# Float32r weight units of 1024 columns, Winograd products accumulated in PSUM, a second tile written ahead of the norm's sum, in a hybrid decoder layer on one core

## The chip, the cores and the metric

The kernel runs on one core of a Trainium2 chip. The metric is the device time of one execution in microseconds (us), lower is better. Engines are named as in the profile: PE is TensorE (PEld its weight loads), DVE is VectorE, ACT is ScalarE, POOL is GpSimd and SP the queue that issues most DMAs.

## The reference

One decoder layer over 512 tokens of width 1024, in float32:

```python
x = x + 0.5 * swiglu(rms_norm(x, ffn1_norm), w_gate, w_up, w_down)     # FFN1, inner width 2816
h = rms_norm(x, mix_norm)
proj = h @ w_in                                                        # RWKV, attention and gate columns
y_rwkv = rwkv7_branch(...)                                             # a recurrence over the tokens, 8 heads of 64
y_att  = attention_branch(...)                                         # sliding window of 128, 8 query heads, 2 key heads
merged = gate_rwkv * (y_rwkv @ w_branch_rwkv) + gate_att * (y_att @ w_branch_attn)
x = x + merged @ w_out
x = x + 0.5 * swiglu(rms_norm(x, ffn2_norm), w_gate2, w_up2, w_down2)  # FFN2
x = rms_norm(x, final_norm)
# swiglu(h) = (silu(h @ w_gate) * (h @ w_up)) @ w_down
```

## The kernel before

**Stages.** The five stages follow each other on the core: the start (transposes of x, the norm's sum, the first FFN1 tiles), FFN1, mix1 (projections, the RWKV recurrence and attention, interleaved), mix2 (branches, gates, `w_out`), FFN2 with the final norm. Activations are kept transposed, features on the 128 partitions and 512 tokens along a row, as eight tiles.

**Products in three passes.** Every float32 product is three float32r matmuls (`mm3`): high part by high part, and the low part of each factor by the high part of the other. So each weight tile is loaded raw (`wr`, or `wx`), its high part `wh` is cast on ACT (L176) and its low part `wl`, raw minus high, is subtracted on DVE (L177, in `split_w`). A raw unit holds `WU` = 512 columns on 128 partitions, 256 KB, and each of the tags `wr`, `wh`, `wl` has three buffers for each of two streams, "a" and "b" (gate and up weights, or even and odd tiles).

**FFN tiles.** The inner width of an FFN is 22 tiles of 128 features. Most are made in pairs (`PAIRS`: 9 pairs in FFN1, tiles 4 to 21, and 11 in FFN2, all tiles). `ffn_pair` makes a pair's gate and up by a scheme of seven products in place of eight (Strassen and Winograd): tokens in two halves of 256, the contraction in two, the two tiles of the pair as two. Sums of the activations (`block_sums`, tags `xt`, `th`, `tl`) are made once for each FFN and shared by its pairs; sums of the weights (`S`, in `wx` buffers) are made for each pair, at L399: four sums, of which `SUMS = (1, 0, 1, 1)` puts three on POOL and one on DVE, each done for gate and for up. A pair's seven products are each 24 matmuls of 256 columns for gate and up together, 168 in all. Each product has its own PSUM tile (`sm`); seven additions on DVE (L399, `xt<-s,sm` and the like) and one copy on ACT (L416) combine them into `x0` and `x1`. `act` then multiplies by the norm's factor `rs` (L449), applies SiLU on ACT (L451), multiplies gate by up (L452) and splits the result into `h` (cast L204, subtraction L205).

**The start.** FFN1's first four tiles are made singly, with 48 matmuls of 512 columns each (eight contraction tiles by three passes, for gate and for up). The first tile's matmuls are written between the transposes of x. The second's weights are loaded and split early (`nextw`); its matmuls are written in `ffn_h`, behind `rs_finish`, which sums the squares over the features with a matmul against ones (L291) and makes `rs` from it. The scheduler may still place matmuls ahead of the sum, as the order below shows. Tiles three and four follow, then the pairs.

**Order.** Where the code sets `pe, v, s` to `InOrder`, the instructions keep the order in which they are written; elsewhere a scheduler places each instruction by its own estimates. In mix1 the matmul jobs (`JOBS`) run in one lane beside lanes for the recurrence and attention; a job's weights are split `AHEAD` = 4 units before use, and `LOE = (1, 0, 0)` puts one in three of their low subtractions on POOL in place of DVE.

## Time and profile before

| what | before |
|---|---|
| device time, median of three runs | 1190.36 us |
| the three runs | 1187.4, 1190.36, 1190.53 us |
| profiled execution: its time | 1189.17 us |
| profiled execution: span in the trace | 1187.4 us |
| mean granted clock of TensorE | 0.987 of full speed |
| busy PE, DVE, ACT, POOL over the span | 1138.7 (96%), 936.5 (79%), 603.7 (51%), 296.2 (25%) us |
| matmuls | 7386 |

The span is the profiled execution from its first to its last instruction; the 1.8 us between it and the execution's time lie around it. PE is busy for nearly the whole span, so the question in each stage is how often PE stood still, and at what rate its matmuls started. Busy shares are averages over stages that have different limits. Records of pipelined matmuls overlap, so the rate of a stretch is read from the number of matmuls that started in it.

### The profile page before, as it was taken

Reading aid. Unit: us, or ns where it says so; the run is one execution under the profiler, and the core shown is the slowest. Engines: PE = TensorE matmul, PEld = TensorE weight load, DVE = VectorE, ACT = ScalarE, POOL = GpSimd, SP = SyncE. Lnnn points to the kernel's source line nnn. Section 1 sums busy time; section 2 is a strip of 40 time slices with the busy share of each in tenths; the row PEclk is TensorE's granted clock in tenths of the full one; section 3 lists DMA queues with packets and bytes.
Section 4 is the critical chain, followed back from the end, with each engine's and each line's share of the span. In section 5 each row is a group of like instructions: output and inputs, shape, how many; then the busy total and the mean of one; then the engine's idle time right before and its main releaser. Section 6 shows DMA issues by size and latency. Waiting matters only on the chain.

```text
span 1187.4 us, 20295 instructions
## 1 busy us (share of the span) xinstructions
PE 1138.7 (96%) x7386; PEld 959.6 (81%) x7386; DVE 936.5 (79%) x1544; ACT 603.7 (51%) x1215; POOL 296.2 (25%) x260
## 2 busy tenths in 40 slices
...
GB/s 235 51 90 146 68 81 102 130 107 81 74 105 170 172 136 57 107 69 95 105 89 136 91 149 113 233 159 66 90 115 134 80 72 94 127 119 81 80 107 71
DMA packets 224597, 130.16 MB, mean 110 GB/s; under 512 B 39248, under 2 KB 205969, under 8 KB 224497
## 3 DMA queue, kind: packets, MB, share of 16 engines
...
q14 instruction: 43, 0.34, 0.1%
...
## 4 chain that ended last, share of the span: by engine, by line
PE 69%; DVE 20%; issue 4%; ACT 3%; DMA 3%; SPq 0%; POOL 0%; DVEq 0%; ACTq 0%; POOLq 0%
PE sm L201 12%; PE sm L200 12%; PE sm L199 11%; PE mm L199 9%; PE mm L200 9%; PE mm L201 8%; PE sm L78 5%; DVE wl L177 5%; DVE pr L916 2%; DVE wx L399 1%; PE sm L68 1%; DVE xt L399 1%; DVE t L449 1%; DVE t L452 1%; ACT wh L176 1%
## 5 line engine op out<-in xcount | busy, mean ns | idle before, releaser
L176 ACT CAST wh<-wr 128x512 fp32r<-128x512 f32 (+1 forms) x282 | 172.1, 612 | 245.4 <-PE mm L200 104.7
L177 DVE TENSOR_TENSOR wl<-wr,wh 128x512 fp32r<-128x512 f32 (+1 forms) x257 | 202.2, 791 | 91.0 <-ACT wh L176 90.3
L399 POOL TENSOR_TENSOR wx<-wr,wx 128x512 f32<-128x512 f32 x80 | 127.8, 1598 | 350.5 <-DVE wl L177 209.1
L176 ACT CAST wh<-wx 128x512 fp32r<-128x512 f32 x200 | 120.6, 619 | 141.5 <-PE sm L200 56.3
L201 PE MATMUL sm<-th,wl 128*128 128x256 f32 x640 | 181.6, 284 | 9.9 <-DVE wl L177 9.8
L199 PE MATMUL sm<-th,wh 128*128 128x256 f32 x640 | 180.2, 282 | 0.0
L200 PE MATMUL sm<-tl,wh 128*128 128x256 f32 x640 | 180.2, 282 | 0.0
L177 DVE TENSOR_TENSOR wl<-wx,wh 128x512 fp32r<-128x512 f32 x200 | 164.2, 851 | 14.2 <-ACT wh L176 14.2
L199 PE MATMUL sm<-xh,wh 128*128 128x256 f32 (+2 forms) x536 | 159.5, 298 | 0.0
L201 PE MATMUL sm<-xh,wl 128*128 128x256 f32 (+2 forms) x536 | 158.4, 296 | 0.6 <-DVE wl L68 0.3
L200 PE MATMUL sm<-xl,wh 128*128 128x256 f32 (+2 forms) x536 | 158.2, 295 | 0.5 <-DVE xl L263 0.5
L199 PE MATMUL mm<-xh,wh 128*128 128x512 f32 x304 | 128.1, 421 | 2.7 <-DVE g L1270 2.1
L201 PEld LDWEIGHTS sm<-th,wl 128*128 128x128 f32 x640 | 120.5, 188 | 12.5 <-DVE wl L177 12.5
L200 PE MATMUL mm<-xl,wh 128*128 128x512 f32 x304 | 124.5, 410 | 0.0
L201 PE MATMUL mm<-xh,wl 128*128 128x512 f32 x304 | 123.5, 406 | 0.0
L199 PEld LDWEIGHTS sm<-th,wh 128*128 128x128 f32 x640 | 120.7, 189 | 0.0
L200 PEld LDWEIGHTS sm<-tl,wh 128*128 128x128 f32 x640 | 120.6, 188 | 0.0
L200 PEld LDWEIGHTS sm<-xl,wh 128*128 128x128 f32 (+1 forms) x536 | 102.6, 191 | 4.2 <-issue 0.8
L201 PEld LDWEIGHTS sm<-xh,wl 128*128 128x128 f32 (+1 forms) x536 | 102.6, 191 | 4.0 <-DVE wl L68 0.8
L199 PEld LDWEIGHTS sm<-xh,wh 128*128 128x128 f32 (+1 forms) x536 | 102.7, 192 | 3.6 <-issue 0.8
L399 POOL TENSOR_TENSOR wx<-wx 128x512 f32<-128x512 f32 x40 | 60.0, 1500 | 113.4 <-DMA wx<-in_ffn_w_gate_dram 75.3
L199 PEld LDWEIGHTS mm<-xh,wh 128*128 128x128 f32 x304 | 58.1, 191 | 19.5 <-issue 2.6
...
## 6 DMA issues: line engine op xcount, KB each, us to landing
...
```

Of the source, the lines that this page charges most:

```text
L68: return lambda *a, **k: self.tc.keep_in_program_order(f(*a, **k))
L78: self.pe.matmul(out, lhsT=lhsT, rhs=rhs, **k)
L176: s.copy(out=hi[:, :n], in_=raw[:, :n])
L177: (e or v).tensor_tensor(out=lo[:, :n], in0=raw[:, :n], in1=hi[:, :n].bitcast(F32), op=ALU.subtract)
L199: pe.matmul(acc, lhsT=ah, rhs=bh, start=(first and k == 0), stop=False)
L200: pe.matmul(acc, lhsT=ah, rhs=bl, start=False, stop=False)
L201: pe.matmul(acc, lhsT=al, rhs=bh, start=False, stop=(last and k == n - 1))
L399: e.tensor_tensor(out=o, in0=a, in1=b, op=op)
L449: v.tensor_tensor(out=sv, in0=gate, in1=rs if len(gate.shape) == 2 else rs.rearrange("p (a c) -> p a c", a=2), op=ALU.mult)
L452: v.tensor_tensor(out=sv, in0=sv, in1=up, op=ALU.mult)
L916: v.tensor_tensor(out=pv_[:, m], in0=a_[:, m].unsqueeze(2).broadcast_to(sh), in1=b_[:, m].rearrange("p u c -> p c u").unsqueeze(1).broadca ...
```

## The change

Four edits go together.

1. A weight unit holds 1024 columns. In a pair it holds a product's gate and up weights side by side; in single tiles all eight contraction tiles; in FFN2's down product two tiles. The two streams become one, with three buffers of each kind (the same bytes). `wx` goes from six buffers of 512 to five of 1024. Units shorter than 1024 columns (w_branch_rwkv, w_branch_attn) leave the rest of their buffer unused.
2. In a pair, products that share an addend are accumulated in one PSUM tile (`pa` takes four products, `pc` two, `pb` one). Copies of the intermediate states of `pa` and `pc` are made on ACT, and three additions on DVE remain. The order of the products changes, and the sign of one activation sum with it.
3. The second tile's 48 matmuls are written as `pnext` ahead of `rs_finish`, into PSUM tiles of another tag (`mm`).
4. In mix1 a job's weights are one unit in place of two, `AHEAD` goes from 4 units to 2, and `LOE` goes: all low subtractions are on DVE.

The core of the diff:

```diff
-WU = 512
-WB = {"a": (3, 3, 3), "b": (3, 3, 3)}
+WU = 1024
+WB = (3, 3, 3)
...
-AHEAD = 4
-LOE = (1, 0, 0)
+AHEAD = 2
...
+    def wtile(which):
+        return wpool.tile([P, WU], F32 if which == 0 else F32R, tag=("wr", "wh", "wl")[which],
+                          name=("wr", "wh", "wl")[which], bufs=WB[which])
+
+    def load_raw(src, nk, nc_, raw=None, o=0):
+        raw = raw or wtile(0)
+        dma.dma_start(out=raw[:, o:o + nk * nc_].rearrange("p (k c) -> p k c", c=nc_), in_=src)
         return raw
-    def split_w(raw, nk, nc_, st, e=None):
-        n = nk * nc_
-        nb = WB[st]
-        hi = wpool.tile([P, WU], F32R, tag="wh" + st, name="wh", bufs=nb[1])
-        lo = wpool.tile([P, WU], F32R, tag="wl" + st, name="wl", bufs=nb[2])
-        s.copy(out=hi[:, :n], in_=raw[:, :n])
-        (e or v).tensor_tensor(out=lo[:, :n], in0=raw[:, :n], in1=hi[:, :n].bitcast(F32), op=ALU.subtract)
-        return (hi[:, :n].rearrange("p (k c) -> p k c", c=nc_),
-                lo[:, :n].rearrange("p (k c) -> p k c", c=nc_))
-
-    def load_cols(w, c0, ncols, k0=0, k1=KT, st="a", raws=None, e=None):
+    def split_w(raw, nk, nc_, hl=None, o=0):
+
+        hi, lo = hl or (wtile(1), wtile(2))
+        c = slice(o, o + nk * nc_)
+        s.copy(out=hi[:, c], in_=raw[:, c])
+        v.tensor_tensor(out=lo[:, c], in0=raw[:, c], in1=hi[:, c].bitcast(F32), op=ALU.subtract)
+        return [tuple(t_[:, o + i * nc_:o + (i + 1) * nc_] for t_ in (hi, lo)) for i in range(nk)]
...
+    pnext = [psmm("a"), psmm("b")]
+    for j in (0, 1):
+        mm3(pnext[j], nextw[j], xhl)
...
-        v.tensor_tensor(out=a_[:, 1, :], in0=x1[:, hi_], in1=x1[:, lo_], op=ALU.subtract)
+        v.tensor_tensor(out=a_[:, 1, :], in0=x1[:, lo_], in1=x1[:, hi_], op=ALU.subtract)
...
-        raw = []
-        for st, w in zip("ab", ws):
-            w = w.rearrange("(j k p) c -> p j k c", p=P, k=2)
-            q = {}
-            for m in (0, 1):
-                for k in (0, 1):
-                    c = slice((f + m) * P, (f + m + 1) * P)
-                    if m == 0:
-                        q[m, k] = load_raw(w[:, :, k, c], KT // 2, P, st)
-                    else:
-                        q[m, k] = slot("wx", (P, WU))
-                        dma.dma_start(out=q[m, k].rearrange("p (k c) -> p k c", c=P), in_=w[:, :, k, c])
-            raw.append(q)
+        def load(m, k):
+            r = slot("wx", (P, WU)) if m else wtile(0)
+            for j, w in enumerate(ws):
+                load_raw(w.rearrange("(j k p) c -> p j k c", p=P, k=2)[:, :, k, (f + m) * P:(f + m + 1) * P], KT // 2, P,
+                         r, j * KT // 2 * P)
+            return r
         def tt(e, o, a, b, op=ALU.add):
             e.tensor_tensor(out=o, in0=a, in1=b, op=op)
-        def prod(which, c):
-            o = pssm("ab"[cnt[0] % 2])
-            cnt[0] += 1
+        def prod(o, w_, c, first=False, last=True):
+
+
+            l_, b = split_w(w_, KT, P), b_(c)
+            n = KT // 2
             for j in (0, 1):
-                mm3(o[:, j * HT:(j + 1) * HT], parts(which(j), j), b_(c))
-            return o
-
-        def parts(r, j):
-            h_, l_ = split_w(r, KT // 2, P, "ab"[j])
-            return [(h_[:, k, :], l_[:, k, :]) for k in range(KT // 2)]
-
-        cnt = [0]
+                acc = o[:, j * HT:(j + 1) * HT]
+                for k in range(n):
+                    (ah, al), (bh, bl) = l_[j * n + k], b[k]
+                    for i, (x_, y_) in enumerate(((ah, bh), (ah, bl), (al, bh))):
+                        pe.matmul(acc, lhsT=x_, rhs=y_, start=first and j == 0 and k == 0 and i == 0,
+                                  stop=last and k == n - 1 and i == 2, skip_group_check=True)
+
         E = [(v, g)[n] for n in SUMS]
+        w00, w10, w11, w01 = (load(*mk) for mk in ((0, 0), (1, 0), (1, 1), (0, 1)))
+        S = slot("wx", (P, WU))
+        tt(E[0], S, w10, w11)
+
+        pa, pc = pssm("a"), pssm("b")
+        prod(pa, w00, 4, first=True)
         s1 = slot(s1tag[0], name="s1")
-        p_ = prod(lambda j: raw[j][0, 0], 4)
-        s.copy(out=s1, in_=p_)
-        p_ = prod(lambda j: raw[j][0, 1], 5)
+        s.copy(out=s1, in_=pa)
+        prod(pc, S, 0, first=True)
+        m5 = slot("s5")
+        s.copy(out=m5, in_=pc)
+        tt(E[1], S, S, w00, ALU.subtract)
+        prod(pa, S, 1)
+        s2 = slot(s1tag[1], name="s2")
+        s.copy(out=s2, in_=pa)
+        pb = pssm("b")
+        prod(pb, w01, 5, first=True)
         x0 = slot("xt", (P, 2, T))
-        tt(v, x0[:, 0], s1, p_)
-        S = [slot("wx", (P, WU)) for _ in (0, 1)]
-        for j in (0, 1):
-            tt(E[0], S[j], raw[j][1, 0], raw[j][1, 1])
-        p5 = prod(lambda j: S[j], 0)
-        for j in (0, 1):
-            tt(E[1], S[j], S[j], raw[j][0, 0], ALU.subtract)
-        p_ = prod(lambda j: S[j], 1)
-        tt(v, s1, s1, p_)
-        for j in (0, 1):
-            tt(E[2], raw[j][1, 0], raw[j][0, 0], raw[j][1, 0], ALU.subtract)
-        p_ = prod(lambda j: raw[j][1, 0], 2)
+        tt(v, x0[:, 0], s1, pb)
+        tt(E[2], w10, w00, w10, ALU.subtract)
+        prod(pa, w10, 2)
         x1 = slot("xt", (P, 2, T))
-        tt(v, x1[:, 0], s1, p_)
-        tt(v, s1, s1, p5)
-        tt(v, x1[:, 1], x1[:, 0], p5)
-        p_ = prod(lambda j: raw[j][1, 1], 3)
-        tt(v, x1[:, 0], x1[:, 0], p_, ALU.subtract)
-        for j in (0, 1):
-            tt(E[3], S[j], raw[j][0, 1], S[j], ALU.subtract)
-        p_ = prod(lambda j: S[j], 6)
-        tt(v, x0[:, 1], s1, p_)
+        tt(v, x1[:, 1], m5, pa)
+        tt(E[3], S, w01, S, ALU.subtract)
+        prod(pc, S, 6)
+        tt(v, x0[:, 1], s2, pc)
+        prod(pa, w11, 3)
+        s.copy(out=x1[:, 0], in_=pa)
         return x0, x1
...
-                for u in ((0,) if c == "b" else (0, 1)):
-                    ahead.append((what, u, "ab"[count % 2], load_cols(
-                        w_branch_attn[0] if c == "b" else win, COLS[c] + i * P, P, 4 * u, 4 * u + 4, st="ab"[count % 2],
-                        e=(v, g)[LOE[(2 * count + u) % len(LOE)]])))
+                ahead.append((what, "ab"[count % 2], load_cols(
+                    w_branch_attn[0] if c == "b" else win, COLS[c] + i * P, P, 0, 4 if c == "b" else KT)))
...
-            mm3(pr_, load_cols(w_branch_rwkv[0], k * P, P, 0, 4, st=sx), xhl[0:4])
+            mm3(pr_, load_cols(w_branch_rwkv[0], k * P, P, 0, 4), xhl[0:4])
...
-            for f in range(nf):
-                wd += load_cols(ffn2_w_down[0], dh * 512, 512, f0 + f, f0 + f + 1, st="ab"[f % 2])
+            for f in range(0, nf, 2):
+                wd += load_cols(ffn2_w_down[0], dh * 512, 512, f0 + f, f0 + f + 2)
```

Lines of the changed kernel lie a little further down: the split's cast and subtraction are L178 and L179 there, a pair's sums and additions L401, the sum over the features L293, `rs` L300, `act`'s two products L453 and L456, the subtraction of `split` L204.

Around the norm's sum PE's program reads as follows before: the end of 38 matmuls of 512 columns (24 of the second tile, for one of its two weights, and the first 14 of the third; `xh` and `xl` are the high and low parts of the activations), the sum over the features, and the first of the second tile's other 24:

```order
L199 MATMUL sm<-xh_127,wh 128x512
L200 MATMUL sm<-xl_135,wh 128x512
L201 MATMUL sm<-xh_127,wl 128x512
L199 MATMUL sm<-xh_128,wh 128x512
L200 MATMUL sm<-xl_136,wh 128x512
L291 MATMUL sm<-t,ones 128x512
L199 MATMUL sm<-xh_124,wh 128x512
L200 MATMUL sm<-xl_132,wh 128x512
```

After the change it reads so: the end of the second tile's 48 matmuls (`mm`), the sum, and the first matmuls of the third tile (`sm`):

```order
L198 MATMUL mm<-xh_128,wh 128x512
L199 MATMUL mm<-xl_136,wh 128x512
L200 MATMUL mm<-xh_128,wl 128x512
L198 MATMUL mm<-xh_129,wh 128x512
L199 MATMUL mm<-xl_137,wh 128x512
L200 MATMUL mm<-xh_129,wl 128x512
L293 MATMUL sm<-t,ones 128x512
L198 MATMUL sm<-xh_122,wh 128x512
L199 MATMUL sm<-xl_130,wh 128x512
```

Of the 144 matmuls of tiles two to four, 48 stand ahead of the sum now, where 38 stood, and 96 behind it, where 106 stood; the last 24 are the fourth tile's up product in both.

On DVE, at the start, the program behind `rs` reads so before; rows with `xT` and `fn1c` and with `tl` make the activation sums, L449, L452 and `h` are `act` of the first three tiles, and `wl` is a half unit of the fourth tile's weights:

```order
L449 TENSOR_TENSOR t<-sm,rs 128x512 x2
L364 SCALAR_TENSOR_TENSOR xt<-xt,fn1c 128x256
L356 TENSOR_TENSOR xt<-xT 128x256
L357 TENSOR_TENSOR xt<-xT 128x256
L364 SCALAR_TENSOR_TENSOR xt<-xT,fn1c,xt 128x256
L177 TENSOR_TENSOR wl<-wr,wh 128x512
L452 TENSOR_TENSOR t<-t,sm 128x512 x2
L449 TENSOR_TENSOR t<-sm,rs 128x512
L205 TENSOR_TENSOR h<-t,h 128x512
L205 TENSOR_TENSOR tl<-xt,th 128x768
L205 TENSOR_TENSOR h<-t,h 128x512
L452 TENSOR_TENSOR t<-t,sm 128x512
```

and so after the change:

```order
L453 TENSOR_TENSOR t<-sm,rs 128x512
L453 TENSOR_TENSOR t<-mm,rs 128x512
L453 TENSOR_TENSOR t<-sm,rs 128x512
L204 TENSOR_TENSOR tl<-xt,th 128x256
L372 SCALAR_TENSOR_TENSOR xt<-xT,fn1c,xt 128x256 x2
L456 TENSOR_TENSOR t<-t,sm 128x512
L456 TENSOR_TENSOR t<-t,mm 128x512
L456 TENSOR_TENSOR t<-t,sm 128x512
L204 TENSOR_TENSOR h<-t,h 128x512
L372 SCALAR_TENSOR_TENSOR xt<-xt,fn1c 128x256
L204 TENSOR_TENSOR h<-t,h 128x512
L179 TENSOR_TENSOR wl<-wr,wh 128x1024
```

The low half of the fourth tile's up weights (the last row) stands behind three products by `rs`, three by up, and two splits now, as one subtraction of 1024.

In FFN2 a piece of a pair reads so on DVE before (`wl` are weight subtractions, `wx` a weight sum, the rows with `sm` additions from PSUM, the rest `act` of the tiles before):

```order
L399 TENSOR_TENSOR wx<-wx,wr 128x512
L399 TENSOR_TENSOR xt<-s_8944,sm 128x512
L177 TENSOR_TENSOR wl<-wx,wh 128x512
L449 TENSOR_TENSOR t<-xt,rs 128x512 x2
L399 TENSOR_TENSOR wx<-wx,wr 128x512
L177 TENSOR_TENSOR wl<-wx,wh 128x512
L452 TENSOR_TENSOR t<-t,xt 128x512 x2
L399 TENSOR_TENSOR xt<-s_9228,sm 128x512
L205 TENSOR_TENSOR h<-t,h 128x512
L177 TENSOR_TENSOR wl<-wx,wh 128x512
L205 TENSOR_TENSOR h<-t,h 128x512
L177 TENSOR_TENSOR wl<-wx,wh 128x512 x5
```

and after the change so:

```order
L179 TENSOR_TENSOR wl<-wx,wh 128x1024 x2
L401 TENSOR_TENSOR xt<-s_8410,sm 128x512
L179 TENSOR_TENSOR wl<-wx,wh 128x1024
L401 TENSOR_TENSOR xt<-s_8440,sm 128x512
L179 TENSOR_TENSOR wl<-wr,wh 128x1024
L401 TENSOR_TENSOR xt<-s_8471,sm 128x512
L453 TENSOR_TENSOR t<-xt,rs 128x512
L179 TENSOR_TENSOR wl<-wx,wh 128x1024
L456 TENSOR_TENSOR t<-t,xt 128x512
L401 TENSOR_TENSOR wx<-wx,wr 128x1024
L204 TENSOR_TENSOR h<-t,h 128x512
L453 TENSOR_TENSOR t<-xt,rs 128x512
```

Counted over a pair, seven subtractions of 1024 stand there for 14 of 512, one weight sum of 1024 for two of 512, and three additions from PSUM for seven. On ACT a pair has seven casts of 1024 for 14 of 512, and four copies from PSUM for one; on POOL three sums of 1024 for six of 512. The matmuls of a pair stay 168.

On SP, at the passage from mix1 to mix2, all eight loads of w_branch_rwkv stood ahead of the run of six loads of the gates `g`; after the change five do, and the other three stand behind it.

## Rows read from the trace of the kernel before

**Rows 1.** Windows of the whole core, by stage: us, then each engine, PE clock, DMA share, GB/s.

```profile
66.50:385.00 318.50, 313.18 (x2074) 285.25 (x2073) 260.69 (x382) 139.48 (x243) 84.80 (x60) 1.00 0.37 105
...
435.00:742.00 307.00, 296.40 (x2147) 211.81 (x2147) 236.44 (x519) 173.47 (x448) 59.66 (x54) 0.97 0.40 101
...
830.00:1187.40 357.40, 343.58 (x2363) 318.26 (x2362) 284.91 (x413) 158.65 (x277) 97.29 (x62) 0.99 0.32 97
```

**Rows 2.** PE's waits in FFN1's stretch: us in total, times, longest.

```profile
PE sm L201 <- DVE wl L177: 3.1, 3, 1.2
PE mm L199 <- ACT h L204: 1.2, 1, 1.2
```

**Rows 3.** PE's waits in FFN2's stretch.

```profile
PE sm L201 <- DVE wl L177: 6.6, 8, 1.2
```

**Rows 4.** The chain that ended last in 24:67: start, us, instruction.

```profile
38.86 2.09 PE sm L291 x2
...
47.53 0.34 DVE rs L298
...
59.70 0.50 PE sm L201
```

**Rows 5.** Windows of the start.

```profile
33.40:39.00 5.60, 0.59 (x3) 0.17 (x2) 5.60 (x9) 3.33 (x7) 2.72 (x2) 0.78 0.06 18
39.00:44.20 5.20, 5.20 (x12) 3.45 (x13) 3.47 (x8) 3.65 (x5) 0.00 (x0) 0.59 0.07 18
44.20:66.50 22.30, 22.00 (x97) 17.84 (x97) 21.07 (x36) 14.03 (x25) 1.30 (x1) 1.00 0.20 58
```

**Rows 6.** Windows of two stretches of FFN2.

```profile
830.00:848.00 18.00, 18.00 (x153) 18.00 (x153) 17.02 (x23) 11.30 (x19) 7.97 (x6) 1.00 0.37 104
...
869.40:891.00 21.60, 20.11 (x167) 19.70 (x166) 21.57 (x30) 10.76 (x19) 9.40 (x7) 1.00 0.34 98
```

**Rows 7.** DVE in order of time, a pair of FFN2: start, us, instruction.

```profile
869.45 1.78 DVE L177 TENSOR_TENSOR wl<-wx,wh 128x512 fp32r<-128x512 f32 x1
...
875.87 1.28 DVE L452 TENSOR_TENSOR t<-t,xt 128x512 f32<-128x512 f32 x2
...
878.27 0.67 DVE L399 TENSOR_TENSOR xt<-s,sm 128x512 f32<-128x512 f32 x1
878.87 1.18 DVE L205 TENSOR_TENSOR h<-t,h 128x512 fp32r<-128x512 f32 x1
879.97 4.78 DVE L177 TENSOR_TENSOR wl<-wx,wh 128x512 fp32r<-128x512 f32 x6
```

**Rows 8.** POOL in order of time, same stretch.

```profile
868.93 1.75 POOL L399 TENSOR_TENSOR wx<-wx 128x512 f32<-128x512 f32 x1
...
877.88 1.62 POOL L399 TENSOR_TENSOR wx<-wr,wx 128x512 f32<-128x512 f32 x1 [5.50 <-DVE wl L177]
...
887.66 1.30 POOL L399 TENSOR_TENSOR wx<-wx 128x512 f32<-128x512 f32 x1 [5.27 <-DMA wx<-in_ffn_w_gate_dram]
```

**Rows 9.** Groups of instructions by line and shape: busy, mean ns.

```profile
L176 ACT CAST wh<-wr 128x512 fp32r<-128x512 f32 x272 | 167.9, 619 | 240.1 <-PE mm L200 101.7 <-PE sm L201 59.2 <-PE sm L200 52.7
...
L204 ACT CAST th<-xt 128x768 fp32r<-128x768 f32 x8 | 6.7, 834 | 4.2 <-DVE xt L364 4.2
...
L1188 DVE TENSOR_TENSOR S<-S,sm 128x1024 f32<-128x1024 f32 x4 | 4.9, 1216 | 0.1
```

**Rows 10.** The same over 385:742, the low subtractions.

```profile
L177 DVE TENSOR_TENSOR wl<-wr,wh 128x512 fp32r<-128x512 f32 x52 | 39.6, 764 | 11.3 <-ACT wh L176 10.8 <-issue 0.2
L177 POOL TENSOR_TENSOR wl<-wr,wh 128x512 fp32r<-128x512 f32 x24 | 34.7, 1447 | 99.9 <-ACT wh L176 97.8 <-PE mm L201 2.1
```

**Rows 11.** PE's waits in mix1 (435:742).

```profile
PE sm L78 <- DVE BK L857: 3.6, 3, 2.4
```

**Rows 12.** PE's waits in mix2 (742:830).

```profile
PE mm L199 <- DVE g L1270: 2.1, 3, 0.9
```

**Rows 13.** Windows of mix2.

```profile
742.00:790.00 48.00, 43.97 (x190) 33.97 (x189) 37.47 (x51) 30.43 (x58) 14.18 (x10) 1.00 0.74 223
```

More of the change, by code (lines that the diff above doesn't have):

```diff
@@ L188, in load_cols @@
             n = min(step, k1 - k)
-            raw = raws.pop(0) if raws else load_raw(view[:, k:k + n, c0:c0 + ncols], n, ncols, st)
-            hi, lo = split_w(raw, n, ncols, st, e)
-            r += [(hi[:, i, :], lo[:, i, :]) for i in range(n)]
+            r += split_w(load_raw(view[:, k:k + n, c0:c0 + ncols], n, ncols), n, ncols)
         return r
@@ L225, in hybrid_layer_kernel @@
     xv = x[0].rearrange("(b p) d -> p b d", p=P)
-    fn1 = slot("fn1", (P, P))
+    fn1 = slot("t")[:, 0:P]
     dma.dma_start(out=fn1[0:KT, :], in_=ffn1_norm[0].rearrange("(n p) -> n p", p=P))
     xtok = []
-    first = {}
+    first, firsts = [], []
     def load_x(j):
@@ L234, in load_x, with load_first @@
         xtok.append(t_)
-    def load_first(which, w, u, st):
-        view = w.rearrange("(k p) c -> p k c", p=P)
-        first.setdefault(which, []).append(load_raw(view[:, 4 * u:4 * u + 4, 0:P], 4, P, st))
+    def load_first(j, u):
+        view = (ffn1_w_gate, ffn1_w_up)[j][0].rearrange("(k p) c -> p k c", p=P)
+        if j == 0:
+            first.append(wtile(0))
+        load_raw(view[:, 4 * u:4 * u + 4, 0:P], 4, P, first[u], 4 * P * j)
     load_x(0)
-    load_first("g", ffn1_w_gate[0], 0, "a")
+    load_first(0, 0)
     load_x(1)
-    load_first("u", ffn1_w_up[0], 0, "b")
+    load_first(1, 0)
     load_x(2)
     load_x(3)
-    load_first("g", ffn1_w_gate[0], 1, "a")
-    load_first("u", ffn1_w_up[0], 1, "b")
+    load_first(0, 1)
+    load_first(1, 1)
     vps = pssm()
@@ L305, in first_split @@
     def first_split(j):
-        wgu[j] += load_cols(None, 0, P, 0, 4, st="ab"[j], raws=first["gu"[j]])
+        if j == 0:
+            firsts.append((first.pop(0), (wtile(1), wtile(2))))
+        wgu[j] += split_w(firsts[-1][0], 4, P, firsts[-1][1], 4 * P * j)
     def first_mm(k):
@@ L363, in block_sums @@
         for i, (b0, b1) in enumerate(((x1[:, hi_], t_[:, 0, :]), (x1[:, hi_], a_[:, 2, :]), (a_[:, 1, :], t_[:, 0, :]))):
-            v.scalar_tensor_tensor(out=t_[:, 1 + i, :], in0=b0, scalar=g1, in1=b1, op0=ALU.mult, op1=ALU.subtract)
+            v.scalar_tensor_tensor(out=t_[:, 1 + i, :], in0=b0, scalar=g1, in1=b1, op0=ALU.mult,
+                                   op1=ALU.add if i == 2 else ALU.subtract)
         split(t_[:, 1:, :], h_[:, 1:, :], l_[:, 1:, :])
         return h_, l_
-    tb, late, s1tag = [], [], ["g"]
+    tb, late, s1tag = [], [], ["g", "s2"]
     def flush(n=0):
@@ L481, in hybrid_layer_kernel @@
     for hi_, (f0, nf) in enumerate(GROUPS):
-        hh = ffn_h(ffn1_w_gate[0], ffn1_w_up[0], f0, nf, PAIRS[0], [pgu, nextw] if hi_ == 0 else None)
+        hh = ffn_h(ffn1_w_gate[0], ffn1_w_up[0], f0, nf, PAIRS[0], [pgu, pnext] if hi_ == 0 else None)
         if hi_ == 0:
```

41 lines of the change are left out of this document (18 added, 23 removed).

## The prediction

> **What bounds the kernel now.** I read the windows by stage first. PE is busy for 313.18 of 318.5 us in FFN1, 296.40 of 307 in mix1 and 343.58 of 357.4 in FFN2 [rows 1], at a granted clock of 0.97 to 1.00. So the number of matmuls bounds the kernel, and the change leaves that number as it is: a pair stays 168 matmuls. What can be won is time in which PE stands still or runs at a lower clock. The waits of PE say where that is. In FFN1 it waits for low weight parts from DVE for 3.1 us in 3 waits and for one `h` for 1.2 us [rows 2]; in FFN2 it waits for nothing but low parts, 6.6 us in 8 waits [rows 3]. So in the pairs DVE is the engine that runs late: in one stretch of FFN2 it is busy for 21.57 of 21.6 us [rows 6]. The second place is the start. The chain of work goes through the sum over the features at 38.86 us [rows 4], and in the windows around it PE has 0.59 us of work in 5.6 us, then 12 matmuls in 5.2 us at a clock of 0.59 [rows 5], about half of the 2.4 GHz level.
>
> **The start.** Of the 5.6 us before the sum PE idles for 5.0. After the change ten more matmuls stand ahead of the sum. At the rate behind it (97 matmuls in 22.3 us, 0.23 us each [rows 5]) they fill 2.3 of these 5.0 us. Behind the sum the ten were run at the low clock: with the sum they took 5.2 us [rows 5], and at full rate ten would be 2.3. I expect the squares to be summed 1 to 3 us earlier, since the scheduler has fewer single units on DVE there, and the clock not to fall as far. Then the third tile starts near 37.2 us, where at 44.2 the same 96 matmuls were left before: 7 us ahead. But DVE does not follow. `rs` came at 47.53 [rows 4]; I leave it there, since the sums of the activations now stand ahead of it on DVE. Behind it the order has the three `act`s' products and two splits, and then the fourth tile's up weights, as one subtraction. These are eight instructions of 512 at 0.60 us (two take 1.28 with the overlap of the records [rows 7]), 4.8, six smaller ones at the 0.34 of `rs` [rows 4], 2.0, and the subtraction of 1024, 1.14 (below): 8 us, and some 1.5 for SiLU between. So the fourth tile's last 24 matmuls, which need that part, start near 57.0 and end 5.6 us later at 62.6, where the tile ended at 66.5 (the edge of the window [rows 5]). That is **-4 us**. It is -7 if DVE keeps up, -1 if `rs` comes 3 us later.
>
> **The pairs.** Before, DVE has 29 instructions of 512 for a pair: 14 low parts, two weight sums, seven additions, six of `act`. At 0.60 us that is 17.4. In the stretch of rows 6 it took 21.6 for about as many (x30), so 4.2 us went to something else. The timeline says to what: a low part next to a POOL sum took 1.78 us, where two instructions of that size by themselves took 1.28 [rows 7, 8]. POOL did seven sums there [rows 6], so a sum costs DVE 0.6 to 0.7 us, or about 0.5 us per us of POOL's work (1.30 for a sum by itself [rows 8]). PE needs less: 153 matmuls start in 18.00 us [rows 6], 0.1176 each, 19.8 for a pair. A pair like that runs 1.8 us behind; single tiles and down products let DVE catch up, so that PE shows only the 12 waits of rows 2 and 3, 3.1 + 1.2 + 6.6 = 10.9 us idle. I add 0.15 us to each for the overlap that a restarted pipeline loses (an estimate: a little more than one matmul of 0.1176): 12.7 us is all that can come back.
>
> After, DVE has seven low parts and one weight sum of 1024 and nine instructions of 512. No such subtraction is in the trace. The addition of 1024 columns with a PSUM operand takes 1.216 [rows 9], with the 0.08 of recorded overlap 1.14; twice the 0.60 would be 1.20. I take 1.14, since it is the row of the same size: 8 x 1.14 + 9 x 0.60 = 14.5 us. POOL has three sums of 1024 in place of six of 512: 3 x 2.5 = 7.5 us, if 1024 costs a little less than twice 1.30 (twice the 1.62 of a disturbed one is 3.2). At 0.5 us per us they hold DVE up for 4.0. That is 18.6 against PE's 19.8: DVE is ahead, and most waits go. ACT has seven casts of 1024. 512 columns cost 619 ns and 768 cost 834 [rows 9], which makes 1.05 for 1024; with four copies and four instructions of `act` at 0.62 it needs 12.3 of 19.8 us, so its three additional copies cost nothing as long as PSUM is read within one product (24 x 0.1176 = 2.8 us), which the next product in another tile covers. I take **-10.5 us** (-8 to -12.7): some wait at the beginning of each group stays, as the first unit of 1024 comes later than one of 512.
>
> **mix1.** Before, DVE makes 52 low parts of 512 and POOL 24 [rows 10]; after, all are on DVE as 34 of 1024 and 8 of 512 (the branch weights). On DVE 34 x 1.14 + 8 x 0.60 = 43.6 instead of 52 x 0.60 = 31.2, 12 us more. What POOL held up goes: the low parts average 764 ns [rows 10] where a DVE instruction of 512 by itself is recorded with 670 [rows 7], and the short instructions of the lanes lose as well; at 0.67 for each of 24, 16 us. So DVE gains some 4 us on balance, of 236 in 307 [rows 1]. On the path are the lanes of the recurrence, for which PE waits up to 2.4 us at a time [rows 11]; a block of 1.14 in front of their short instructions is worse than one of 0.60. I take **-1 us**, with -6 to +12 (all 12 us on the path).
>
> **mix2.** Units of 512 now use half a buffer, and only three raw buffers are there, so three of the eight w_branch_rwkv loads (256 KB) are issued among the gates' loads, in a window that moves 223 GB/s [rows 13], 1.2 us each. PE waits there for the gates' product for 2.1 us [rows 12]. I take one load more on the path: **+1 us** (-1 to +5).
>
> **The sum.** The profiled execution took 1189.17 us, within 0.1% of the median 1190.36. 1189.2 - 4 - 10.5 - 1 + 1 = 1174.7, so 1175.
>
> **Rivals.** *Exclusion (B).* DVE and POOL may shut each other out whenever both read two SBUF operands. For it: the low part at 869.45 ends at 871.23, 0.55 us (one instruction) behind the POOL sum that ends at 870.68 [rows 7, 8]; the split at 878.87 (1.18 us) ends 0.55 behind POOL's end at 879.50; but the addition with a PSUM operand at 878.27, inside the same POOL sum, took 0.67 [rows 7]. Then DVE's two-operand work and POOL's add up. Before, 22 x 0.60 + 6 x 1.27 = 20.8 per pair, 4% under the 21.6 seen; after, 8 x 1.14 + 6 x 0.60 + 3 x 2.5 = 20.2, with 4% 21.0. Over PE's 19.8 that leaves 1.2 where 1.8 was: two thirds of the waits stay, the pairs give 4.2 instead of 10.5, and the kernel 1181. The removed additions, which had a PSUM operand, are then just those that POOL never held up. Against it: the 20.2 without the 4% is nearly PE's time.
> The Trainium skill, page "SBUF — State Buffer", section "Who interferes with whom", states such a rule: the port pair that VectorE shares with GpSimd is an exclusive lock, a VectorE instruction with two SBUF inputs contends with a GpSimd one that reads SBUF, and one with at most one such input does not. By it the time is 1181 rather than 1175. The three rows just named agree with it.
>
> *Blocks in front of the lanes (C), slower.* In mix1 every low part of 1024 stands 0.54 us longer before the lanes' instructions than one of 512. If each of the 34 delays the path by 0.6 us, 20 us are lost: 1189.2 - 4 - 10.5 + 20 + 1 = 1195. It decides from about 0.55 us per unit (18.7 in all) on. For it: PE waits for DVE there [rows 11]. Against: DVE is busy for 236 of 307 us [rows 1], and a wait of a lane is mostly filled by the projections' matmuls.
>
> *Losses eat the gain (D), same.* B's smaller gain, 4.2, with 8 us lost in mix1 and mix2 and 4 won at the start: 1189.
>
> *mix1 gains too (E).* If the lanes, free of POOL's 24 blocks, win 6 us or more, and the start 5 to 7: 1189.2 - 6 - 12 - 6 + 1, near 1166.
>
> **Chances.** A (the sum) 0.50, B 0.22, E 0.10, D 0.10, C 0.08. A measurement of this kernel can tell about 0.3%, 3.6 us, from no change. Faster, then, is A, B and E, 0.82; same D, 0.10; slower C, 0.08. The likeliest case has 1170 to 1180 (its pairs' and start's bounds). The range reaches from E's lower end, 1163 (all four terms at their best: 1189.2 - 7 - 12.7 - 6), to D's middle, 1188; outside are C, half of D and a little of E, some 0.16.
>
> **What would show it.** Start: the sum over the features comes with a short wait, the clock in the windows behind it stays near 1.00, and the pairs begin near 62.6; if they begin at 66 or later, DVE was the path all along. Pairs: PE's waits for low parts in FFN1 and FFN2 fall from 9.7 us to 3 or less, a pair takes 19.8 us, and DVE is below 95% busy; if POOL's sums of 1024 and the low parts beside them stretch by 1 us and more and the waits stay at 6 us, B holds. mix1: its window lasts 306 us; 312 or more would be C's beginning. mix2: the wait for the gates' product is 2 to 4 us. I am wrong if mix1 grows by 10 us, if DVE's 1024 subtraction costs over 1.2 us by itself, or if products that share a PSUM tile wait for ACT's copies.

## The result, and the profile after

The changed kernel took 1172.48 us in the median (1169.41 to 1175.4, 4 runs) against 1188.88 for the kernel before in the same runs; the ratio is 0.9864, with a 95% interval of 0.9826 to 0.9902. The profiled execution has a span of 1172.6 us where 1187.4 was, 14.8 us less. 1175 was forecast; but one of the four terms of the sum did not come, and the others made up for it.

To see where the time went I read five boundaries from PE's order of time in every trace: the first matmul of the pairs (in kernel 2 the beginning of their unbroken run; one stands alone at 59.2), the first of FFN1's last down product, the 31st of the 96 with `yas` (the attention branch's product, near mix1's end), the first pair matmul behind FFN2's norm sum (3.65 to 3.71 us behind FFN2's very first one), the end. The table has the time between them, in us; a difference taken from it can be 0.1 off by rounding. The kernels further down are in it.

| kernel | start | FFN1 | mix1 | mix2 | FFN2 | span |
|---|---|---|---|---|---|---|
| before | 66.6 | 276.0 | 390.8 | 95.7 | 358.2 | 1187.4 |
| changed | 66.4 | 270.5 | 387.9 | 96.1 | 351.7 | 1172.6 |
| changed, a second execution | 66.0 | 270.5 | 384.3 | 96.4 | 351.7 | 1168.8 |
| 1: ffn1_norm in its own tile | 62.3 | 270.5 | 382.3 | 97.0 | 351.6 | 1163.7 |
| 2: low parts as two of 512 | 70.1 | 272.6 | 378.1 | 95.4 | 356.0 | 1172.1 |
| 3: no accumulation in PSUM | 66.9 | 278.7 | 384.3 | 98.2 | 362.4 | 1190.5 |
| 4: a third of mix1's low parts on POOL | 66.6 | 270.5 | 394.9 | 95.6 | 351.7 | 1179.2 |
| 5: before + second tile ahead | 62.4 | 275.2 | 388.0 | 97.3 | 357.7 | 1180.5 |
| 6: 1 + halves in mix1 | 63.8 | 270.5 | 378.2 | 98.0 | 351.9 | 1162.3 |
| 7: 1 + weight sums on DVE | 59.2 | 270.2 | 384.0 | 93.7 | 349.7 | 1156.9 |
| 8: before, low parts all on DVE | 66.7 | 274.8 | 378.2 | 97.0 | 358.0 | 1174.6 |
| 9: 1 + 6 + 7 | 59.1 | 270.1 | 378.6 | 94.6 | 349.7 | 1152.2 |

**The pairs.** The windows of two whole pairs of FFN2 after the change, from the first matmul of a pair to the first of the next, columns as in [rows 6] (the engines are PE, PEld, DVE, ACT, POOL):

```profile
860.58:880.60 20.02, 20.02 (x171) 20.02 (x170) 19.06 (x18) 11.54 (x16) 9.38 (x3) 1.00 0.35 106
880.60:900.79 20.19, 20.19 (x172) 20.19 (x171) 18.59 (x19) 11.73 (x17) 6.09 (x2) 1.00 0.43 129
```

These two pairs take 20.0 and 20.2 us, with PE busy throughout. Pairs differ, so I take the mean of nine, from FFN2's second to its tenth: 20.16 us with DVE busy for 18.05 (14.8 to 20.3), where before the change it was 20.91 with DVE busy for 20.31. A window's count includes matmuls that began ahead of it, which is why 171 stand where a pair has 168. PE's waits in FFN1 and the rest of the start, then in FFN2, stand for [rows 2] and [rows 3]:

```profile
PE sm L200 <- DVE wl L179: 1.8, 1, 1.8
PE mm L200 <- DVE wl L179: 1.0, 1, 1.0
PE mm L198 <- ACT wh L178: 0.9, 1, 0.9
```
```profile
PE sm L413 <- DVE wl L179: 0.9, 2, 0.6
PE sm L413 <- ACT s L424: 0.3, 1, 0.3
PE sm L413 <- DVE xt L401: 0.3, 1, 0.3
```

In FFN2 PE waits 0.9 us for low parts where it waited 6.6, in FFN1's pairs no more (the 1.8 are the start's fourth tile, the 1.0 and 0.9 lie behind the last pair). FFN1 lost 5.5 us and FFN2 6.6, 12.1 in all.

**The start** gave 0.3 us only. The first row of PE's order of time, before and after the change, then from SP's after the change the load that it waited for:

```profile
2.47 0.24 PE L249 MATMUL sm<-ident,fn 8*128 8x8 f32 x1 [2.47 <-DMA fn<-in_ffn_norm_dram]
12.27 0.24 PE L251 MATMUL sm<-ident,t 8*128 8x8 f32 x1 [12.27 <-DMA t<-in_ffn_norm_dram]
```
```profile
4.52 1.56 SPq L171 DMA_DIRECT2D wr<-in_ffn_w_up_dram  x1
6.12 1.12 SPq L226 DMA_DIRECT2D t<-in_ffn_norm_dram  x1
7.28 0.39 SPq L171 DMA_DIRECT2D wr<-in_ffn_w_gate_dram  x1
```

PE begins at 12.27 us; before, the same transpose of ffn1_norm began at 2.47. The load was SP's first and is its eighth now, issued behind 2.5 MB of x and weights (three loads of 512 KB, four of 256). The edit that moved it is a line of the diff that stands in no part of the forecast:

```diff
-    fn1 = slot("fn1", (P, P))
+    fn1 = slot("t")[:, 0:P]
```

The windows of the start (to the first tile's end, to the sum over the features, to the pairs) show the other half:

```profile
12.20:29.60 17.40, 17.26 (x82) 14.04 (x83) 12.46 (x19) 12.81 (x20) 6.32 (x9) 1.00 0.84 219
29.60:42.10 12.50, 11.57 (x51) 9.12 (x50) 10.14 (x16) 9.00 (x16) 6.39 (x3) 1.00 0.55 153
42.10:66.40 24.30, 22.55 (x99) 18.14 (x98) 24.27 (x39) 17.04 (x25) 3.31 (x1) 1.00 0.18 53
```

The clock is 1.00 in all three, where 0.59 stood [rows 5], and PE stands still for 0.9 us ahead of the sum where it stood for 5.0. So the tile written ahead did its part, and the late beginning ate it.

**mix1** became shorter by 2.9 us in this execution, and by 6.5 in the second one of the same kernel. The difference between the two executions is the clock, which the part on experiment 8 takes up.

### The profile page after: what moved, and what is told of

Read it like the earlier page. It is cut to its first block, busy times and chain, and to the rows that moved or that the text cites. A ratio compares the mean times of both kernels' runs of the same rounds, so it can differ in the third digit from the quotient of the medians.

```text
span 1172.6 us, 19053 instructions
## 1 busy us (share of the span) xinstructions
PE 1131.1 (96%) x7386; PEld 954.5 (81%) x7386; DVE 886.0 (76%) x1234; ACT 600.0 (51%) x1040; POOL 248.1 (21%) x175
## 4 chain that ended last, share of the span: by engine, by line
PE 77%; DVE 12%; ACT 3%; DMA 3%; issue 2%; POOL 1%; SPq 1%; ACTq 0%; DVEq 0%; POOLq 0%
PE sm L413 30%; PE mm L198 10%; PE mm L200 10%; PE mm L199 10%; PE sm L77 6%; PE sm L200 3%; PE sm L198 3%; PE sm L199 3%; DVE wl L179 3%; ACT wh L178 1%; PE sm L67 1%; DVE pr L916 1%; DVE xt L372 1%; PE sm L81 1%; DMA t<-gd 1%
## 5 line engine op out<-in xcount | busy, mean ns | idle before, releaser
L179 DVE TENSOR_TENSOR wl<-wr,wh 128x1024 fp32r<-128x1024 f32 (+2 forms) x149 | 215.6, 1447 | 70.2 <-ACT wh L178 69.4
L178 ACT CAST wh<-wr 128x1024 fp32r<-128x1024 f32 (+2 forms) x149 | 147.5, 990 | 203.4 <-PE mm L199 88.5
L401 POOL TENSOR_TENSOR wx<-wr,wx 128x1024 f32<-128x1024 f32 x40 | 116.2, 2904 | 371.4 <-DVE wl L179 244.6
L179 DVE TENSOR_TENSOR wl<-wx,wh 128x1024 fp32r<-128x1024 f32 x100 | 157.5, 1582 | 27.1 <-ACT wh L178 26.6
L178 ACT CAST wh<-wx 128x1024 fp32r<-128x1024 f32 x100 | 105.0, 1050 | 131.8 <-PE sm L413 80.3
L413 PE MATMUL sm<-xh,wl 128*128 128x256 f32 x480 | 136.0, 283 | 0.9 <-DVE wl L179 0.9
L413 PE MATMUL sm<-xh,wh 128*128 128x256 f32 x480 | 136.0, 283 | 0.0
L413 PE MATMUL sm<-xl,wh 128*128 128x256 f32 x480 | 135.7, 283 | 0.0
L413 PEld LDWEIGHTS sm<-xh,wl 128*128 128x128 f32 x480 | 91.8, 191 | 1.3 <-DVE wl L179 1.3
L413 PEld LDWEIGHTS sm<-xh,wh 128*128 128x128 f32 x480 | 91.7, 191 | 0.5 <-issue 0.2
```

The source lines that it names most:

```text
L178: s.copy(out=hi[:, c], in_=raw[:, c])
L179: v.tensor_tensor(out=lo[:, c], in0=raw[:, c], in1=hi[:, c].bitcast(F32), op=ALU.subtract)
L401: e.tensor_tensor(out=o, in0=a, in1=b, op=op)
L413: pe.matmul(acc, lhsT=x_, rhs=y_, start=first and j == 0 and k == 0 and i == 0, stop=last and k == n - 1 and i == 2, skip_group_check=True)
```

## The experiments

**1. ffn1_norm in its own tile.**

```diff
-    fn1 = slot("t")[:, 0:P]
+    fn1 = slot("fn1", (P, P))
```

> The changed kernel with the load of ffn1_norm in a tile of its own again, so that it is the first DMA on SP instead of the eighth. Theory (the start lost what the tile written ahead won, because PE's first transpose waited for this load until 12.27 us, where it began at 2.47 before): the first tile ends near 24.4 instead of 29.6, the sum over the features comes near 36.5, the pairs begin near 61.5 instead of 66.4, and the kernel takes 4 to 5 us less, near 1168. Rival (the start is bound by DVE, which has the sums of the activations and rs to make whatever PE does): the pairs still begin at 66 and the time stays at 1172.

1165.6 us (6 runs), ratio to before 0.9809 (0.9761 to 0.9858). The load is SP's first again, and PE's, DVE's and ACT's programs are otherwise the same. The pairs begin at 62.3: 4.1 us won, as the theory has it. The rival falls. The further 2.8 us of the median are not the load's; mix1's 382.3 differs from 387.9 by the clock, but for 0.5 us (below). The chain of work of this kernel says what sets the start's end now:

```profile
33.48 3.19 POOL t L278
36.69 0.69 DVE t L278
...
48.54 0.34 DVE rs L300
...
55.92 1.14 DVE wl L179
57.11 0.50 PE sm L200
```

The chain goes through the sum of squares (POOL, 3.19 us for 512 columns), `rs` at 48.5 and the fourth tile's up weights, which end at 57.06. The forecast had the last two at 47.5 and 57.0.

**2. Low parts as two subtractions of 512.**

```diff
-        v.tensor_tensor(out=lo[:, c], in0=raw[:, c], in1=hi[:, c].bitcast(F32), op=ALU.subtract)
+        for b in range(o, o + nk * nc_, 512):
+            q = slice(b, min(b + 512, o + nk * nc_))
+            v.tensor_tensor(out=lo[:, q], in0=raw[:, q], in1=hi[:, q].bitcast(F32), op=ALU.subtract)
```

> The changed kernel with each low-part subtraction of 1024 as two of 512 on DVE; buffers, casts and products stay. Theory (DVE's columns and additions count, not the number of its instructions): 0.4 us more DVE time per pair (16 x 0.60 against 8 x 1.14, of 19.6), the pairs keep their 19.6 us, 1170 to 1175. Rival (the 1024 wide instruction itself won the time): pairs at 20.4 us or more and 1180 or over. Rival for mix1 (blocks of 1.14 us in front of the lanes cost time there): mix1 gets 3 us or more shorter.

1174.95 us (4 runs), ratio 0.9876 (0.9826 to 0.9926). The whole is as the theory says, but by compensation: the start lost 3.7 us, FFN1 and FFN2 6.5, and mix1 won 9.8, of which 6.8 are a drop of the clock that the changed kernel had there (experiment 8). So the expectation that pairs keep their time fell: the mean of the nine pairs is 20.61 us for 20.16. The additions from PSUM come late now. A wait of PE in FFN2, a whole pair, and the group of the subtractions from `wx`, five of a pair's seven (busy time, mean ns):

```profile
PE sm L415 <- DVE xt L403: 3.4, 5, 0.9
```
```profile
856.92:878.05 21.13, 20.24 (x170) 20.07 (x169) 20.79 (x26) 11.57 (x16) 8.20 (x3) 1.00 0.33 100
```
```profile
L181 DVE TENSOR_TENSOR wl<-wx,wh 128x512 fp32r<-128x512 f32 x200 | 186.4, 976 | 20.6 <-ACT wh L178 20.5
```

DVE is nearly full in this pair (20.79 of 21.13 us). Over the nine pairs it is busy for 19.30 us a pair, 1.25 more than with 1024, not the 0.4 that the instructions' own durations give. The group accounts for it: its 200 halves were busy for 186.4 us, where 100 of 1024 took 157.5 (shown in experiment 7), 1.4 us more a pair. Two halves by themselves take 1.28 [rows 7], 128 us for all, so POOL's sums held the halves up for some 58 us, against 35 with 1024. The 1024 wide subtraction is worth some 6 us in the pairs; in mix1 it costs 3.0, less the drop.

**3. No accumulation in PSUM.** Each product has its own tile again, and the additions are on DVE:

```diff
-        prod(pa, w00, 4, first=True)
-        s.copy(out=s1, in_=pa)
-        prod(pc, S, 0, first=True)
-        s.copy(out=m5, in_=pc)
...
+        s.copy(out=s1, in_=one("a", w00, 4))
+        p5 = one("b", S, 0)
+        tt(v, s2, s1, one("a", S, 1))
+        tt(v, x0[:, 0], s1, one("b", w01, 5))
+        tt(v, x1[:, 0], s2, one("a", w10, 2))
+        tt(v, s2, s2, p5)
+        tt(v, x1[:, 1], x1[:, 0], p5)
+        tt(v, x0[:, 1], s2, one("b", S, 6))
+        tt(v, x1[:, 0], x1[:, 0], one("a", w11, 3))
```

> The changed kernel with a PSUM tile for each of the seven products again, seven additions on DVE and one copy on ACT, in the new order of products and with units of 1024. Theory (DVE's load decides: four additions of 0.60 more): 14.5 + 2.4 + 4 held up by POOL = 20.9 us per pair against PE's 19.6, waits of PE come back and the kernel takes 5 to 9 us more, 1177 to 1181. Rival (units of 1024 with shared buffers won the time, additions are cheap since POOL does not hold them up): 1172 to 1175.

1192.29 us (10 runs), ratio 1.0011 (0.998 to 1.0042): all of the gain is gone, 20 us against the changed kernel. The direction is the theory's, its size was put too low by a factor of two to four: 20.9 against 19.6 us a pair is 1.3, times 20 is 26 us, and I had expected 5 to 9. A pair's window and, from DVE's and then POOL's order of time, the three sums of this pair:

```profile
998.30:1020.95 22.65, 21.26 (x171) 20.31 (x169) 22.61 (x22) 9.91 (x12) 10.80 (x3) 1.00 0.31 93
```
```profile
1004.91 0.68 DVE L204 TENSOR_TENSOR h<-t,h 128x512 fp32r<-128x512 f32 x1
1005.51 0.69 DVE L451 TENSOR_TENSOR t<-t,xt 128x512 f32<-128x512 f32 x1
1006.11 1.22 DVE L179 TENSOR_TENSOR wl<-wr,wh 128x1024 fp32r<-128x1024 f32 x1
1007.25 0.68 DVE L204 TENSOR_TENSOR h<-t,h 128x512 fp32r<-128x512 f32 x1
1007.85 3.43 DVE L179 TENSOR_TENSOR wl<-wx,wh 128x1024 fp32r<-128x1024 f32 x1
1011.20 0.67 DVE L401 TENSOR_TENSOR s<-s,sm 128x512 f32<-128x512 f32 x1
1011.80 3.04 DVE L179 TENSOR_TENSOR wl<-wx,wh 128x1024 fp32r<-128x1024 f32 x1
1014.76 0.67 DVE L401 TENSOR_TENSOR xt<-s,sm 128x512 f32<-128x512 f32 x1
1015.35 2.83 DVE L179 TENSOR_TENSOR wl<-wx,wh 128x1024 fp32r<-128x1024 f32 x1
```
```profile
1005.07 5.13 POOL L401 TENSOR_TENSOR wx<-wr,wx 128x1024 f32<-128x1024 f32 x1 [10.62 <-DVE wl L179]
1011.35 2.40 POOL L401 TENSOR_TENSOR wx<-wx 128x1024 f32<-128x1024 f32 x1 [1.16 <-DVE wl L179]
1013.83 3.27 POOL L401 TENSOR_TENSOR wx<-wr,wx 128x1024 f32<-128x1024 f32 x1
```

DVE is full, 22.61 of 22.65 us (20.37 of 21.38 in the mean of the nine pairs). Each time that a low part meets a POOL sum it ends 1.08 or 1.09 us behind the sum's end (1011.28 behind 1010.20, 1014.84 behind 1013.75, 1018.18 behind 1017.10), which is about its own length (1.14): it did nothing while the sum ran. The three cost DVE 2.2, 1.8 and 1.6 us over an undisturbed 1.22. The sum at 1005.07 in turn took 5.13 us instead of 2.40: its last 2.40 us begin at 1007.80, when the last of four DVE instructions that read two SBUF operands (1004.91 to 1007.25) was about to end. The Trainium skill, page "SBUF — State Buffer", section "SBUF: two separate sides", has it so that whichever starts first, a VectorE instruction with two SBUF inputs or a GpSimd one that reads SBUF, gets the shared pair of ports for the whole instruction, and the other fully blocks. The low parts that waited for a sum agree. That a waiting sum let four DVE instructions pass is shown by these rows and not by that sentence.

Against the kernel before, this one is slower by 2.7 us in FFN1 and 4.2 in FFN2. So units of 1024 without the accumulation, in the new order of products and with the shared buffers, lose 7 us in the pairs, and the accumulation wins 19.

**4. A third of mix1's low parts on POOL again**, as units of 1024 (`e` is the engine of the subtraction, handed through `load_cols`):

```diff
-                    w_branch_attn[0] if c == "b" else win, COLS[c] + i * P, P, 0, 4 if c == "b" else KT)))
+                    w_branch_attn[0] if c == "b" else win, COLS[c] + i * P, P, 0, 4 if c == "b" else KT, e=(g, v, v)[count % 3])))
```

> The changed kernel with every third unit's low part in mix1 on POOL again, as 1024 columns. Theory (DVE without POOL's blocks beside it won the 3 us by which mix1 became shorter): mix1 gets 3 to 6 us longer, 1175 to 1178. Rival (mix1 became shorter by other things, by whole jobs as units or by fewer instructions): no change, or 2 us less since DVE has 10 us less to do there, 1170 to 1173.

1180.71 us (10 runs), ratio 0.9925 (0.9899 to 0.995): 8 us slower than the changed kernel, 7.0 of it in mix1 (drops of the clock take 6.8 us from both). The direction is the theory's, the size a little above its 3 to 6.

**5. The second tile ahead, alone.** The kernel before with

```diff
+    pnext = [psmm("a"), psmm("b")]
+    for j in (0, 1):
+        mm3(pnext[j], nextw[j], xhl)
     rs_finish()
```

> The kernel before with one part of the change: the second tile's 48 matmuls written ahead of the norm's sum. Its own tile for ffn1_norm stays, so PE's first transpose begins at 2.5 us. Theory (the tile written ahead wins 4 us at the start, and nothing else): the pairs begin near 62.5 where they began at 66.6, 4 us less in all, 1184 to 1187 in runs that agree with the profile. Rival (DVE sets the end of the start, so the pairs begin at 66 whatever PE does): no change.

1183.18 us (4 runs) against 1188.51, ratio 0.996 (0.9942 to 0.9979). The pairs begin at 62.4, 4.2 us earlier. The theory holds, and with 1 it closes the account of the start: 4.2 won by the tile, 4.1 lost by the load.

**6. Halves in mix1 alone**, on top of 1 (the loop of 2, with its step handed through `load_cols`, 512 in mix1 and 1024 elsewhere).

> The kernel with ffn1_norm in its own tile, and in mix1 alone the low part of 1024 columns as two subtractions of 512 on DVE; casts, buffers and order of jobs stay. Theory (a block of 1.14 us in front of the lanes' short instructions costs mix1 time; with halves everywhere mix1 had 378.1 us against 387.9): mix1 4 to 8 us shorter than the 382.3 of the same kernel without it, 1158 to 1162. Rival (mix1 varies by that much from one execution and order to another): 1165 to 1168.

1162.75 us (4 runs), ratio 0.9789 (0.9774 to 0.9805), 2.9 us under kernel 1. mix1 has 378.2 us, 4.1 less than there, of which 1.7 are a drop of the clock that kernel 1 had (experiment 8). The 4.1 are the lower end of what was expected, and 1162.75 us lies just above the expected range. The block's width costs time in mix1, but less than 0.1 us for each of its 34 units (2.4 us).

**7. All weight sums of the pairs on DVE**, on top of 1.

```diff
-SUMS = (1, 0, 1, 1)
+SUMS = (0, 0, 0, 0)
```

> The kernel with ffn1_norm in its own tile and all weight sums of the pairs on DVE, none on POOL. Theory (POOL's sums hold DVE's subtractions up for their whole length, so three of 1.14 on DVE cost less than three of 2.4 to 3.3 on POOL; and PE is the bound of the pairs in both): DVE busy 17.9 us of a pair's 19.6 and no subtraction over 1.25 us, the time the same within 2 us, 1164 to 1167. Rival (POOL's sums run beside DVE's work at little cost): DVE at 14.5 + 3.4 + waits over 19.6, pairs of 20 us or more, 1172 or over.

1157.97 us (4 runs), ratio 0.9748 (0.9733 to 0.9763): 7.6 us less than kernel 1 and better than expected. The groups by line say what left, first of the changed kernel, then of this one (busy time, mean ns); a whole pair of this one follows:

```profile
L179 DVE TENSOR_TENSOR wl<-wr,wh 128x1024 fp32r<-128x1024 f32 x124 | 192.7, 1554 | 60.9 <-ACT wh L178 60.4
...
L179 DVE TENSOR_TENSOR wl<-wx,wh 128x1024 fp32r<-128x1024 f32 x100 | 157.5, 1582 | 27.1 <-ACT wh L178 26.6
```
```profile
L179 DVE TENSOR_TENSOR wl<-wr,wh 128x1024 fp32r<-128x1024 f32 x124 | 151.5, 1221 | 55.4 <-ACT wh L178 55.1
...
L179 DVE TENSOR_TENSOR wl<-wx,wh 128x1024 fp32r<-128x1024 f32 x100 | 122.0, 1221 | 21.5 <-ACT wh L178 21.5
```
```profile
846.26:866.29 20.03, 20.03 (x170) 20.03 (x169) 18.38 (x21) 11.57 (x15) 0.00 (x0) 1.00 0.35 106
```

1554 and 1582 ns became 1221. Times 124 and 100 that is 77 us which POOL's 60 sums had held DVE up, 1.3 us each or 3.9 a pair; a sum on DVE itself costs 1.14. In the pairs PE was nearly always the bound in both, so they give only 0.3 + 1.9 us. The start gives 3.0: in kernel 1 POOL's weight sums at 22.09 and 39.42 us each held a DVE instruction up for 2.2 us (3.43 for 1.22, 2.63 for 0.48), and without them `rs` comes 3.0 us earlier. mix2 gives 3.3, where FFN2's first sums fall; PE's waits there for `mg` (1.8 us) and `xk` (1.5) became none and 0.6. mix1 lost 1.7.

**8. The kernel before with all low parts of mix1 on DVE.**

```diff
-LOE = (1, 0, 0)
+LOE = (0, 0, 0)
```

> The kernel before with all low parts of mix1 on DVE, none on POOL; units of 512 as before. Theory (POOL's subtractions in mix1 hold up DVE's short instructions; putting them back cost the changed kernel 7 us there): mix1 3 to 7 us shorter than its 390.8, 1183 to 1187. Rival (with units of 512 DVE's 24 more subtractions cost as much as POOL's blocks): no change, or slower.

1176.37 us (4 runs), ratio 0.9907 (0.9891 to 0.9923): 12.1 us from one number, all of it in mix1 (378.2 against 390.8), more than the theory had. The windows of mix1's first part, of before and of this kernel:

```profile
430.00:450.00 20.00, 17.63 (x111) 14.18 (x110) 17.36 (x25) 7.49 (x14) 2.99 (x3) 0.83 0.43 98
450.00:490.00 40.00, 37.62 (x213) 28.86 (x212) 38.28 (x93) 20.55 (x39) 3.38 (x5) 1.00 0.34 68
490.00:520.00 30.00, 27.97 (x194) 19.10 (x194) 22.60 (x42) 16.09 (x47) 5.75 (x8) 0.77 0.41 99
```
```profile
430.00:450.00 20.00, 19.26 (x132) 15.37 (x131) 18.77 (x39) 12.74 (x23) 0.10 (x1) 1.00 0.50 111
450.00:490.00 40.00, 38.53 (x244) 28.96 (x242) 39.35 (x94) 19.90 (x45) 0.64 (x5) 1.00 0.37 76
490.00:520.00 30.00, 30.00 (x237) 20.74 (x237) 26.19 (x52) 19.95 (x52) 3.04 (x6) 1.00 0.33 85
```

Before, the clock is 0.83 over 20 us and 0.77 over 30: in each window lies a drop, a stretch in which the granted clock is at the lower of its two levels. Each drop stands behind a wait of PE for DVE:

```profile
PE sm L78 <- DVE BK L857: 2.4, 1, 2.4
```
```profile
PE sm L78 <- DVE YT L991: 2.0, 1, 2.0
```

With POOL's blocks gone those waits are gone and the clock is 1.00. Counted as share of the clock times time, the two drops are 3.4 + 6.9 = 10.3 us of the 12.6. The changed kernel has such a drop too, in one place in the one execution, behind a wait for a low part:

```profile
PE mm L200 <- DVE wl L179: 1.0, 1, 1.0
```
```profile
430.00:510.00 80.00, 77.20 (x546) 56.45 (x544) 75.74 (x157) 45.58 (x99) 3.97 (x10) 1.00 0.41 89
...
520.00:540.00 20.00, 18.23 (x151) 11.40 (x150) 14.45 (x38) 7.69 (x23) 1.22 (x2) 0.66 0.45 126
```

It costs 6.8 us by the same count; in the other execution there is a smaller one at another place (3.4), and in kernel 1 one ahead of 380 us (1.7). Less these, mix1 has 381.1, 380.9 and 380.6 us there, and 380.5 in the kernel before. Kernels 2, 6, 8 and 9 have no drop there and 378.1 to 378.6; kernels 3, 5 and 7 have, less their drops, 380.9, 381.2 and 382.3.

Not every such wait is followed by a drop. Kernel 5 has the code of the kernel before in mix1, and in its execution the first of the two waits stands without one; its second wait is followed by a drop as before:

```profile
PE sm L78 <- DVE BK L860: 2.4, 1, 2.4
```
```profile
430.00:445.00 15.00, 12.41 (x100) 9.93 (x101) 14.78 (x28) 8.95 (x16) 0.61 (x2) 1.00 0.46 99
```

So how much of the 12 us hangs on the clock stays open; the count takes it for nearly all. The four runs of this kernel have a granted clock of 0.992 to 0.995 and the seven of the kernel before beside them 0.985 to 0.989, which fits the count. But three other runs of the kernel before, with 0.992 and 0.993, have spans of 1181.9 to 1184.4 us against 1174.5 to 1176.9 for these four: at a like clock some 8 us of difference are left.

**9. Together:** ffn1_norm's own tile, the sums on DVE, halves in mix1.

> What the runs so far point to, together: the changed kernel with ffn1_norm in its own tile, all weight sums of the pairs on DVE, and in mix1 the low parts of 1024 as two subtractions of 512. Theory (the two edits act in different stages, so they add): start and FFN as with the sums on DVE alone (pairs begin near 59, FFN2 349.7 us), mix1 near 378, together 1151 to 1156. Rival (mix1's time is not set by the width of the blocks, and what it won before was spread between executions): 1157 to 1160.

1153.2 us (5 runs), ratio to before 0.9699 (0.9677 to 0.972), 19 us under the changed kernel. The edits add, as the theory has it.

**10. The changed kernel again.**

> The changed kernel as it is, once more, to see how much mix1 and the other stages vary from one execution to another: the start at 66.4, FFN1 and FFN2 within 0.5 us of 270.5 and 351.7, as in three other kernels with the same pairs; mix1 between 382 and 388 if it varies by itself.

1171.11 us (2 runs). Start, FFN1 and FFN2 are the same within 0.4 us; mix1 had 384.3.

## Why the prediction was right, and where not

**The sum** was 14.5 us and the spans differ by 14.8, but the agreement is partly luck: the start gave 3.7 us less than its term, the pairs 1.6 more, mix1 1.9 more (5.5 in the other execution).

**The start (-4; measured -0.3): wrong.** What failed is the sentence that the third tile starts near 37.2 us because ten matmuls more stand ahead of the sum. It took the beginning of PE's work as given. It began 9.8 us later, because a load had moved from SP's first place to its eighth, and the third tile started at 42.1. The order of SP shows that before any run. The mechanism itself held: with the load back the pairs begin at 62.3, with the tile alone at 62.4, and 62.6 was said. That the clock would not fall held as well; that DVE then sets the end, too (kernel 1's chain).

**The pairs (-10.5; measured -12.1): right.** 18.6 us of DVE time were worked out for a pair (the terms as written give 18.3 to 18.5) and 18.05 measured in the mean, with single pairs up to 20.3; 1.14 for the subtraction of 1024 is 1.22 in the records with their overlap; 3.9 us of hold-up a pair were measured for 4.0. PE's 19.8 was low: the 153 matmuls of [rows 6] include some that began ahead of the window, and a pair that PE bounds takes 20.0 us from its first matmul to the next pair's. The parts are not equal: the four additions removed are worth 19 us, and units of 1024 with those additions left in lose 7 (experiment 3).

**Exclusion (B): its mechanism is shown, its price was wrong.** DVE's subtraction and POOL's sum do shut each other out (experiment 3's rows). But adding their full times gave 20.2 to 21.0 us a pair and 1181. By the durations of experiment 7 only 3.9 of the 7.5 us count, and DVE stays under PE. That the rest of POOL's time fell beside DVE's additions and waits is likely, but I have not added it up. In FFN2, 0.9 us of waits were left, not the 6 at which B would have held.

**mix1 (-1; measured -2.9 and -6.5): right in sign, wrong in its parts.** Putting the low parts on DVE is worth 12.6 us in units of 512 (experiment 8), where I had counted 4 us of DVE time and 1 on the path; PE's clock is part of it, how large a part is open. The wider blocks give 2.4 us of it back by themselves (kernel 1's 380.6, which is less its drop, against 378.2 in experiment 6), the drops the rest. Less the drops mix1 did not become shorter at all, 381.1 and 380.9 us against 380.5 before: by the count, what it gave in these executions is time at the higher clock, a term that the forecast did not have. That its sign came out right is partly luck. C's mechanism is therefore real and stayed far below its 0.55 us per unit.

**mix2 (+1; measured +0.4):** as said, but within the spread of kernels 1 and 4 and the second execution, 95.6 to 97.0.
